# Half-size weight chunks, and a unit of its own for emptying a pair of PSUM banks

## The chip, the cores and the metric

The kernel runs on one core of a Trainium2 chip. The metric is the device time of the whole program in microseconds. TensorE is called PE here (PEld: its weight loads), VectorE DVE, ScalarE ACT, GpSimd POOL and SyncE SP, as in the profile. A granted clock of 1.00 is TensorE's upper level of 2.4 GHz, 0.50 the lower one of 1.2 GHz.

## The reference

Two transformer blocks of two layers each, on one sequence of 256 tokens by 1024 features, all in float32. The first block is a mixture of two attentions and a convolved feed-forward network (FFN); the second is an FFN, a "mix" stage and another FFN. Cut to the second block, where most of the steps below lie:

```python
for l in range(2):                                   # second_block
    x = x + 0.5 * swiglu(rms_norm(x, n1[l]), w_gate1, w_up1, w_down1)     # 1024 -> 2816 -> 1024
    proj = rms_norm(x, nm[l]) @ w_in[l] + b_in[l]
    q, k, v, f_logit, xr, gr, g_attn, g_rnn = split(proj)
    y_attn = forgetting_attention(norm(q), norm(k), v, log_sigmoid(f_logit)) @ w_o_attn[l]
    yr = rg_lru(causal_conv(xr), ...) * gelu(gr)      # sigmoid gates, then a scan over the tokens
    y_rnn = yr @ w_o_rnn[l]
    x = x + (sigmoid(g_attn) * y_attn + sigmoid(g_rnn) * y_rnn) @ w_out[l]
    x = x + 0.5 * swiglu(rms_norm(x, n2[l]), w_gate2, w_up2, w_down2)
```

## The kernel before

**Weights.** All weights, about 330 MB, are read once, in one fixed order (`stream`, built by `phase_chunks`). A chunk is 128 partitions by 2048 float32, 1 MB. `issue_dma` (L250) loads a chunk into one of NRAW = 3 raw buffers (L240) from SP's queue, in one transfer, or in two of 512 KB for the row chunks of the down projections. Each product is made out of two or three products of parts, for which every weight is split in two: ACT writes the high part `wh` (`piece_h`, L275), DVE the rest `wl` = raw - wh (`piece_l`, L289), in NP = 4 pieces of 128x512 a chunk. The parts lie in rings of RING = 3 chunks each. `h_open` (L271) lets the split run up to two chunks ahead of the chunk that was taken last (`next_chunk`, L321, sets `done`). A raw buffer is free for the next load when DVE has made the last piece of it.

**Order of work.** The program is unrolled in Python and its order on each engine is written out when it is built. The PE stream is written by straight code (`proj2`, `vpair`, `down2` and so on). Between two products `substep` calls `urgent` (at least one piece of split for the next chunk), `tick` and `fill` (more split if an estimate of the engines' times allows it). `tick` (L350) goes through `active`, a list of units: generators that issue the work of ACT, DVE and POOL on a result (attention rows, gates, emptying of PSUM). A unit is resumed when its inputs are ready by the estimate and its engine is estimated to be at most CAP = 1.4 us ahead of PE, or CAPF = 4.5 us for a unit spawned with `front=True`, which also stands first in the list. Each engine runs its stream in the order so written.

**PSUM.** There are eight banks. `proj2` (L581), a product of 256 output features by 256 tokens, takes two (`wait_for(lambda: bank_any(2))`, L586); they are given back when the unit that uses the result has issued the two additions of `add_parts` (L596) or `add_bias` (L606), which sum the two halves of each bank into SBUF (ACT copies one half, DVE adds the other). That unit stands behind the older units of the list.

**An FFN of the second block.** 22 `proj2` ("up", a chunk each) make 22 tiles of the hidden layer; `evac_swiglu` (L758) turns each into an operand `as` of the down projection. `ffn_order` (L214) puts the down products in between: groups of four hidden tiles for the first 512 output features (half 0), a group when its last tile is two steps old (`lag`, 2; 4 in the first block), and after the last "up" the rest of half 0 and then all of half 1, beginning with the short group of two tiles. In the last group of a half the products are ordered by output tile, so that `boundary` (L708) can add each to `x` and make the operands `xs` of the next stage while PE goes on.

**The mix stage of the second block** (`mix2`, L1433) follows MIX2 (L235). Its later part is: G (gates of the recurrent unit), r0 to r3 and n2, n3 (`proj2` of the same input), A0 to A3, R0 to R3, O0 to O3. r0 to r3 are emptied by four `gelu_unit` (L1393), which stand in the list behind eight gate units and four `lru_unit` (L1371), the recurrence; each then waits for the recurrence, and their products `sp` are the operands of R0 to R3.

**The start.** The first four x tiles and the first two chunks are loaded in pieces of 256 KB in turn, then constants, then chunk by chunk. The squares of x for the first norm are added up on POOL (`add_squares`, L530), and a table of attention biases (`biasT`) is built by POOL's DMAs through DRAM.

Of the kernel before, what the change touches and what calls it, by code (L numbers as in the profile page):

```python
# [25 lines left out]
NG = -(-NF // 4)  # L26
NBLK = 41
# [40 lines left out]
class Estimate:  # L68
# [9 lines left out]
    def key(self, x):  # L78

        w = self.wide.get(x.name)  # L80
        return x.name if w is None else (x.name, 4 * x.offset // w)

    def cost(self, eng, op, out, ins, kw):
# [12 lines left out]
        if eng == "pool":  # L96
            return 149.0 + 2.1 * w
# [47 lines left out]
def kernel(ctx: ExitStack, tc: tile.TileContext, t: dict):  # L145
# [34 lines left out]
    def phase_chunks():  # L180
        for l in range(L):
            wo = t["w_out"]
            at = {"dq0": 0, "dq1": 1, "mq0": 2, "mq1": 3, "dv0": 4, "mv0": 5}
            for step in MIX1.split():
                if step[1] == "o":
                    stream.append(wo[l, 2 * (step[0] == "m") + int(step[2])])
                else:
                    stream.extend(t["w_p1"][l, at[step], i] for i in range(2))
            ffn_chunks(t["w_up"], t["w_down"], l, 4)
        for l in range(L):  # L190
# [3 lines left out]
            for step in MIX2.split():  # L194
                if step == "q0":
                    stream.append(t["w_qf"][l])
                elif step == "G":
                    stream.append(t["w_g"][l])
                elif step in PAIRS:
                    stream.extend(t["w_p2"][l, PAIRS.index(step), i] for i in range(2))  # L200
                elif step[0] == "O":
                    stream.append(half_rows(t["w_out2"][l], *divmod(int(step[1]), 2)))
                elif step[0] in "AR":
                    stream.append(t[{"A": "w_oa", "R": "w_or"}[step[0]]][l, int(step[1])])
                else:
                    stream.append(wi[l, base[step[0]] + int(step[1])])
            ffn_chunks(t["w_gu2"], t["w_d2"], l, 2)

    def half_rows(w, half, g):

        v = w[2 * g:min(2 * g + 2, w.shape[0])].rearrange("c p (k m) -> p c k m", k=2)
        return v[:, :, :, half * 512:(half + 1) * 512]

    def ffn_order(lag):  # L214
# [3 lines left out]
        for j in range(NF):  # L218
            yield "up", j
            while left and 4 * left[0] + 3 + lag <= j:  # L220
                yield "dn", (0, left.pop(0))
        for g in left:
            yield "dn", (0, g)
        for g in [NG - 1, *range(NG - 1)]:
            yield "dn", (1, g)

    def ffn_chunks(u, d, l, lag):
        for what, j in ffn_order(lag):
            stream.append(u[l, j] if what == "up" else half_rows(d[l], *j))
# [10 lines left out]
    NRAW = 3  # L240
    RING = 3
    NP = 4
# [7 lines left out]
    def issue_dma(parts=1, also=None):  # L250
# [7 lines left out]
        if len(stream[c].shape) == 4:  # L258
            rv = r.rearrange("p (c k m) -> p c k m", k=2, m=512)
            for i in range(rv.shape[1]):  # L260
                nc.sync.dma_start(rv[:, i], stream[c][:, i])
# [5 lines left out]
        T["dma"] = max(T["dma"], T["dve"] if c >= NRAW else 0.0) + 2900.0  # L267
# [7 lines left out]
    def piece_h():  # L275
        c, p = divmod(st["h"], NP)
        if p == 0:
            Hs[c] = wpool.tile([P, wide(c)], F32R, tag="wh", bufs=RING, name=nm("wh"))
            Ls[c] = wpool.tile([P, wide(c)], F32R, tag="wl", bufs=RING, name=nm("wl"))
            est.wide[Hs[c].name] = est.wide[Ls[c].name] = wide(c)  # L280
# [18 lines left out]
    def fill():  # L299

        issue_dma()
        while h_open() and st["h"] - st["l"] < 2 * NP:
# [9 lines left out]
    def urgent():  # L312

        if st["l"] < min((st["use"] + 1) * NP, NCHUNK * NP):
# [88 lines left out]
    for x in X:  # L403
        est.wide[x.name] = 4 * S
# [7 lines left out]
    for c in range(2):  # L412
        issue_dma(NP, lambda i: i % 2 == 0 and nc.sync.dma_start(X[2 * c + i // 2], t["x"][2 * c + i // 2]))
    for p in range(4):
        est.R[X[p].name, 0] = est.R[X[p].name, 1] = T0 - 500.0 + 2200.0 * p
    est.R[raws[0].name], est.R[raws[1].name], T["dma"] = T0 + 200.0, T0 + 4600.0, T0 + 5500.0
    nc.sync.dma_start(cst, t["cst"])
    T["dma"] += 1400.0
    issue_dma()
# [25 lines left out]
    def mm3(out, lh, ll, rh, rl, start, stop):  # L445
        pe.matmul(out, lh, rh, start=start, stop=False, skip_group_check=True)
        pe.matmul(out, lh, rl, start=False, stop=False, skip_group_check=True)
        pe.matmul(out, ll, rh, start=False, stop=stop, skip_group_check=True)

# [108 lines left out]

    def proj(R):

        h, l_ = next_chunk(None)
        h3 = h.rearrange("p (k c) -> p k c", k=KT)
        l3 = l_.rearrange("p (k c) -> p k c", k=KT)
# [3 lines left out]
        for k in range(KT):  # L567
            for m in range(2):
                ms = slice(m * P, (m + 1) * P)
                mm3(o[:, m], h3[:, k, ms], l3[:, k, ms], R.high(k), R.low(k),  # L570
# [10 lines left out]
    def proj2(R):  # L581

        h, l_ = next_chunk(None)
        h3 = h.rearrange("p (k c) -> p k c", k=KT)
        l3 = l_.rearrange("p (k c) -> p k c", k=KT)
        wait_for(lambda: bank_any(2))  # L586
        bs = [bank("mm") for _ in range(2)]
        for k in range(KT):
            for m in range(2):
                ms = slice(m * P, (m + 1) * P)  # L590
                mm2(bs[m], h3[:, k, ms], l3[:, k, ms], R.both(k), k == 0, k == KT - 1)
# [4 lines left out]
    def add_parts(t, bs):  # L596

        yield W("act", *bs)
        for m in range(2):
            act.activation(as2(t)[:, m], lo(bs[m]), AF.Copy)  # L600
        yield W("dve", t)
        for m in range(2):
            dve.tensor_add(as2(t)[:, m], hi(bs[m]), as2(t)[:, m])
            unbank()

    def add_bias(t, bs, cols):  # L606

        yield W("act", *bs)
        for m in range(2):
            act.activation(as2(t)[:, m], hi(bs[m]), AF.Identity, bias=cols[m])  # L610
        yield W("dve", t)
        for m in range(2):
            dve.tensor_add(as2(t)[:, m], lo(bs[m]), as2(t)[:, m])
            unbank()

    def vproj(R):

        h, l_ = next_chunk(None)
        h3 = h.rearrange("p (k c) -> p k c", k=KT)
        l3 = l_.rearrange("p (k c) -> p k c", k=KT)  # L620
        w = h3.shape[2]
# [4 lines left out]
        for k in range(KT):  # L626
            for m in range(2):
                ms = slice(m * P, (m + 1) * P)
                mm3(o[m], R.high(k)[:, ms], R.low(k)[:, ms], h3[:, k], l3[:, k],
# [5 lines left out]
    def vpair(R):  # L635
# [3 lines left out]
        for half in range(2):  # L639
            h, l_ = next_chunk(None)  # L640
            h3 = h.rearrange("p (k c) -> p k c", k=KT // 2)
            l3 = l_.rearrange("p (k c) -> p k c", k=KT // 2)
            for kk in range(KT // 2):
                k = half * (KT // 2) + kk
                for tt in range(2):
                    xh, xl = R.high(k)[:, tt * P:(tt + 1) * P], R.low(k)[:, tt * P:(tt + 1) * P]
                    last = k == KT - 1
                    pe.matmul(bs[tt], xh, h3[:, kk], start=k == 0, stop=False, skip_group_check=True)
                    substep()
                    pe.matmul(bs[tt], xl, h3[:, kk], start=False, stop=False, skip_group_check=True)  # L650
                    pe.matmul(bs[tt], xh, l3[:, kk], start=False, stop=last, skip_group_check=True)
                    if not (last and tt):
                        substep()
        return bs

    def down(acc, R, first, last, after=None):

        h, l_ = next_chunk(None)
        h3 = h.rearrange("p (k c) -> p k c", k=2)
        l3 = l_.rearrange("p (k c) -> p k c", k=2)  # L660

        def one(k, m):
            ms = slice(m * P, (m + 1) * P)
            mm3(as2(acc[m // 2])[:, m % 2], h3[:, k, ms], l3[:, k, ms], R.high(k), R.low(k),
                first and k == 0 and m % 2 == 0, last and k == 1 and m % 2 == 1)

        if not last:
            for k in range(2):
                for mh in range(2):
                    for m in range(4 * mh, 4 * mh + 4):  # L670
                        one(k, m)
                        substep()
        else:
            for p in range(4):
                for k in range(2):
                    for m in (2 * p, 2 * p + 1):
                        one(k, m)
# [6 lines left out]
    def down2(acc, R, ks, half_, first, last, after):  # L684

        h, l_ = next_chunk(None)
# [1004 lines left out]
```

## Time and profile before

| | us |
|---|---|
| median of 3 runs | 1897.28 |
| lowest and highest | 1894.22, 1897.31 |
| the profiled execution, its own time | 1893.61 |
| span in its profile | 1891.8 |
| PE busy | 1857.2 |
| ACT busy | 1258.8 |
| DVE busy | 1523.7 |

The span runs from the first to the last instruction; 1.8 us lie around it. PE's busy time is 98% of the span. Matmuls overlap, so one that takes 395 ns by itself costs less in a row of them, and the time of a stage is best read from the chain of work that ended last, where the pieces add up. A profile line names its instruction by its tiles: `mm` and `acc` are PSUM banks, `wh` and `wl` the parts of the weights, `ge` the emptied banks of r0 to r3.

### The profile page before, as it was taken

To read this page: it belongs to the slowest core of one execution; us is meant where nothing else is said; L and a number is where in the kernel's file an instruction comes from. 1 tells how busy PE (TensorE), PEld (TensorE's weight loads), DVE (VectorE), ACT (ScalarE), POOL (GpSimd) and SP (SyncE) were. 2 spreads that over 40 slices of the span, in tenths; PEclk is the share of its full clock that TensorE was granted. 3 is DMA by queue.
4 is the path that set the end of the run, shared out by engine and by line. 5 is a ranking of instruction groups with operands and counts; after the bars stand their busy time and mean duration, and the time that the engine had idled before them with its cause. 6 is when DMAs were issued, how large, how long until landed. Compare 5 with 4: busy or idle time off the path is not lost.

```text
span 1891.8 us, 31179 instructions
## 1 busy us (share of the span) xinstructions
PE 1857.2 (98%) x11446; PEld 1652.2 (87%) x11446; DVE 1523.7 (81%) x3301; ACT 1258.8 (67%) x3123; POOL 69.0 (4%) x98
## 2 busy tenths in 40 slices
PE   8999999999999999999989999999999999899999
PEld 6799998889999888888878888888888888788888
DVE  6889887888988777779977987787777897888775
ACT  6777565877656656567786665566556678866653
POOL 3010001001000000010000100010000000000000
PEclk9999999999999999999998999999999999899999
DMA  9435555443554655464454555555546445455543
GB/s 268 153 113 182 198 168 204 142 157 134 201 179 152 227 195 184 167 227 164 169 179 163 182 189 199 167 201 192 198 156 247 167 156 179 170 184 191 191 157 133
DMA packets 79161, 339.68 MB, mean 180 GB/s; under 512 B 7020, under 2 KB 8084, under 8 KB 48288
## 3 DMA queue, kind: packets, MB, share of 16 engines
q1 hardware_dynamic: 77408, 330.20, 51.1%
q0 software_dynamic: 1456, 7.47, 1.3%
q8 instruction: 90, 1.47, 0.3%
q14 instruction: 63, 0.52, 0.1%
q10 hardware_dynamic: 144, 0.02, 0.0%
HBM read 336.30 MB, written 1.36 MB: 178 GB/s over the span
## 4 chain that ended last, share of the span: by engine, by line
PE 92%; ACT 3%; DVE 3%; DMA 2%; issue 0%; SPq 0%; ACTq 0%
PE mm L112 51%; PE acc L112 23%; PE mv L112 13%; DMA raw<-in_w_p 2%; PE av L112 1%; DVE wl L112 1%; PE s L112 1%; ACT wh L112 1%; PE qt L112 1%; PE pt L112 1%; ACT r L112 1%; ACT th L112 1%; DVE xs L112 0%; DVE z L112 0%; DVE yc L112 0%
## 5 line engine op out<-in xcount | busy, mean ns | idle before, releaser
L112 DVE TENSOR_TENSOR wl<-raw,wh 128x512 fp32r<-128x512 f32 x1272 | 816.2, 678 | 142.0 <-ACT wh L112 132.6
L112 ACT ACTIVATE wh<-raw 128x512 fp32r<-128x512 f32 x1272 | 702.2, 617 | 201.5 <-PE acc L112 85.7
L112 PE MATMUL mm<-xs,wh 128*128 128x256 f32 (+1 forms) x2816 | 745.5, 339 | 2.8 <-DVE xs L112 2.8
L112 PE MATMUL mm<-xs,wl 128*128 128x256 f32 x2112 | 591.4, 280 | 0.0
L112 PEld LDWEIGHTS mm<-xs,wh 128*128 128x128 f32 x2816 | 483.6, 189 | 64.4 <-DVE xs L112 3.6
L112 PEld LDWEIGHTS mm<-xs,wl 128*128 128x128 f32 x2112 | 399.7, 189 | 0.1
L112 PE MATMUL acc<-as,wh 128*128 128x512 f32 x1056 | 369.8, 395 | 0.0
L112 PE MATMUL acc<-as,wl 128*128 128x256 f32 x1056 | 294.9, 279 | 0.0
L112 PE MATMUL mv<-wh,xs 128*128 128x512 f32 (+2 forms) x832 | 255.2, 384 | 0.0
L112 PEld LDWEIGHTS acc<-as,wh 128*128 128x128 f32 x1056 | 198.4, 188 | 46.1
L112 PE MATMUL mm<-hS,wh 128*128 128x512 f32 x512 | 185.8, 406 | 16.7 <-DVE ge L112 16.7
L112 PEld LDWEIGHTS acc<-as,wl 128*128 128x128 f32 x1056 | 199.3, 189 | 0.0
L112 PEld LDWEIGHTS mv<-wh,xs 128*128 128x128 f32 x832 | 149.7, 189 | 26.2 <-ACT xs L112 0.6
L112 PE MATMUL mv<-wl,xs 128*128 128x512 f32 (+2 forms) x416 | 156.1, 375 | 0.0
L112 DVE TENSOR_TENSOR u<-mm,u 128x256 f32<-128x256 f32 x176 | 67.5, 424 | 100.8 <-ACT u L112 100.8
L112 PE MATMUL mm<-hS,wl 128*128 128x256 f32 x512 | 145.1, 283 | 0.0
L112 ACT ACTIVATE u<-mm 128x256 f32<-128x256 f32 x176 | 63.7, 384 | 117.2 <-PE mm L112 116.9
L112 PEld LDWEIGHTS mm<-hS,wh 128*128 128x128 f32 x512 | 98.6, 193 | 40.0 <-issue 17.3
L112 POOL TENSOR_TENSOR sq<-sq,sq 128x256 f32<-128x256 f32 x70 | 55.7, 796 | 1578.1 <-ACT sq L112 1576.3
L112 PEld LDWEIGHTS mm<-hS,wl 128*128 128x128 f32 x512 | 99.0, 193 | 0.1
L112 ACT ACTIVATE as<-u 128x256 fp32r<-128x256 f32 x88 | 36.3, 416 | 82.3 <-DVE u L112 82.3
L112 PEld LDWEIGHTS mv<-wl,xs 128*128 128x128 f32 x416 | 78.5, 189 | 13.3 <-DVE wl L112 0.3
(209 smaller groups left out, 2279.4 us busy)
## 6 DMA issues: line engine op xcount, KB each, us to landing
raw<-in_w_gu SPq DMA_DIRECT2D x88, 1024.0 KB, 4.9
raw<-in_w_up SPq DMA_DIRECT2D x44, 1024.0 KB, 4.9
raw<-in_w_d SPq DMA_DIRECT2D x88, 512.0 KB, 4.6
raw<-in_w_p SPq DMA_DIRECT2D x42, 1024.0 KB, 5.3
raw<-in_w_in SPq DMA_DIRECT2D x34, 1024.0 KB, 4.9
raw<-in_w_down SPq DMA_DIRECT2D x44, 512.0 KB, 4.5
raw<-in_w_out SPq DMA_DIRECT2D x8, 1024.0 KB, 4.9
raw<-in_w_oa SPq DMA_DIRECT2D x8, 1024.0 KB, 4.8
```

Of the source, the lines that this page charges most:

```text
L112: f(*a, **k)
```

## The change

Chunks are halved: every chunk of the stream becomes two of 128x1024 (512 KB, one transfer each), split in NP = 2 pieces of 128x512. NRAW becomes 7 and RING 5, both in half chunks, and the limits of `fill` and `urgent` are doubled in halves, so that they are the same in pieces. Products take the halves one after the other through a generator, `k_chunks`; where the products are ordered by output tile, all halves of the group are taken at once with `list`. The groups of an FFN's down projection are of two hidden tiles instead of four (NG = 11), except the last of half 1, which has two groups at once; half 1 begins with group 0.

`add_parts` and `add_bias` go away. `summed` spawns a unit of its own, with `front=True`, that empties the two banks of a `proj2`; the unit that uses the result polls until it is there.

The squares of the first norm are added on DVE, the pool of working tiles has 43 buffers instead of 41, and the estimate's numbers for POOL and for loads are adapted.

```diff
-NG = -(-NF // 4)
-NBLK = 41
+NG = NF // 2
+NBLK = 43
+    def halves(a):
+        w = a.shape[-1] // 2
+        stream.extend(a[:, i * w:(i + 1) * w] for i in range(2))
...
     def half_rows(w, half, g):
-        v = w[2 * g:min(2 * g + 2, w.shape[0])].rearrange("c p (k m) -> p c k m", k=2)
-        return v[:, :, :, half * 512:(half + 1) * 512]
+        return w[g].rearrange("p (k m) -> p k m", k=2)[:, :, half * 512:(half + 1) * 512]
     def ffn_order(lag):
         left = list(range(NG))
         for j in range(NF):
             yield "up", j
-            while left and 4 * left[0] + 3 + lag <= j:
-                yield "dn", (0, left.pop(0))
+            while left and 2 * left[0] + 1 + lag <= j:
+                yield "dn", (0, (left.pop(0),))
         for g in left:
-            yield "dn", (0, g)
-        for g in [NG - 1, *range(NG - 1)]:
-            yield "dn", (1, g)
+            yield "dn", (0, (g,))
+        for g in range(NG - 2):
+            yield "dn", (1, (g,))
+        yield "dn", (1, (NG - 2, NG - 1))
...
-    NRAW = 3
-    RING = 3
-    NP = 4
+    NRAW = 7
+    RING = 5
+    NP = 2
...
-        while h_open() and st["h"] - st["l"] < 2 * NP:
+        while h_open() and st["h"] - st["l"] < 4 * NP:
...
-        if st["l"] < min((st["use"] + 1) * NP, NCHUNK * NP):
+        if st["l"] < min((st["use"] + 2) * NP, NCHUNK * NP):
...
-            pool.tensor_add(N.ss[0], N.ss[0], sq)
+            (dve if N is norms[0] else pool).tensor_add(N.ss[0], N.ss[0], sq)
...
+    def k_chunks(n=KT, c=2):
+        per = n // c
+        for i in range(c):
+            h, l_ = next_chunk(None)
+            h3 = h.rearrange("p (k c) -> p k c", k=per)
+            l3 = l_.rearrange("p (k c) -> p k c", k=per)
+            for j in range(per):
+                yield i * per + j, h3[:, j], l3[:, j]
...
-    def add_parts(t, bs):
...
-    def add_bias(t, bs, cols):
...
+    def summed(name, bs, cols=None):
+        x = Box()
+        x.t = blk(name)
+        def unit():
+            yield W("act", *bs)
+            for m in range(2):
+                if cols is None:
+                    act.activation(as2(x.t)[:, m], lo(bs[m]), AF.Copy)
+                else:
+                    act.activation(as2(x.t)[:, m], lo(bs[m]), AF.Identity, bias=cols[m])
+            yield W("dve", x.t)
+            for m in range(2):
+                dve.tensor_add(as2(x.t)[:, m], hi(bs[m]), as2(x.t)[:, m])
+                unbank()
+            x.ready = True
+        spawn(unit(), front=True)
+        return x
...
     def down2(...)
-            for m in range(4):
-                for i in range(len(ks)):
-                    one(i, m)
+            w = list(k_chunks(n, len(groups)))
+            for m in range(4):
+                for i, h, l_ in w:
+                    one(i, m, h, l_)
...
-    def gelu_unit(b, j, l, R):
-        ge = blk("ge")
-        yield from add_bias(ge, b, [v1(("bin", l), 32 + 2 * j + m) for m in range(2)])
-        while R.nh < 4:
+    def gelu_unit(x, j, l, R):
+        while not x.ready or R.nh < 4:
             yield POLL
+        ge = x.t
...
-                spawn(gelu_unit(proj2(H_), j, l, R))
+                spawn(gelu_unit(summed("ge", proj2(H_), bias(32 + 2 * j)), j, l, R))
```

## Rows read from the trace of the kernel before

**Rows 1.** the page's span, and its part 1: busy time, share of the span, instructions.
```profile
span 1891.8 us, 31179 instructions
...
PE 1857.2 (98%) x11446; PEld 1652.2 (87%) x11446; DVE 1523.7 (81%) x3301; ACT 1258.8 (67%) x3123; POOL 69.0 (4%) x98
```

**Rows 2.** waits of PE, whole span: what waited for what, us in total, times, longest.
```profile
PE mm L112 <- DVE ge L112: 16.7, 2, 8.4
PE qt L112 <- DVE qn L112: 7.2, 1, 7.2
```

**Rows 3.** windows of 40 us: busy time (instructions) by engine, granted clock, DMA share, GB/s.
```profile
0.00:40.00 40.00, 36.67 (x161) 29.87 (x162) 26.67 (x60) 29.56 (x111) 15.72 (x29) 1.00 0.92 271
40.00:80.00 40.00, 32.66 (x181) 26.09 (x180) 29.21 (x92) 31.80 (x140) 0.00 (x0) 0.91 0.59 169
960.00:1000.00 40.00, 31.63 (x187) 27.93 (x186) 27.76 (x52) 38.52 (x80) 0.00 (x0) 0.91 0.47 161
```

**Rows 4.** the chain of work that ended last: start us, us, what.
```profile
758.25 22.19 PE mm L112 x128
780.43 38.83 PE acc L112 x224
...
996.72 59.55 PE mm L112 x320
...
1623.40 58.63 PE mm L112 x320
```

**Rows 5.** windows of 2 us, PE alone: busy (instructions), granted clock, DMA share, GB/s.
```profile
990.00:992.00 2.00, 0.00 (x0) 1.00 0.50 209
992.00:994.00 2.00, 0.00 (x0) 0.67 0.55 102
```

**Rows 6.** timeline of ACT, 930 to 1045: start, us, instruction.
```profile
991.80 3.01 ACT L112 ACTIVATE ge<-mm,vec 128x256 f32<-128x256 f32 x8
```

**Rows 7.** timeline of DVE, the same stretch.
```profile
996.16 2.07 DVE L112 TENSOR_TENSOR ge<-mm,ge 128x256 f32<-128x256 f32 x6
...
1014.60 1.10 DVE L112 TENSOR_TENSOR sp<-ge,sp 128x256 fp32r<-128x256 f32 x3 [0.88 <-ACT sp L112]
```

**Rows 8.** windows of layer 0's mix stage: columns as in Rows 3.
```profile
960.00:988.40 28.40, 28.36 (x177) 25.11 (x175) 16.26 (x31) 27.96 (x60) 0.00 (x0) 1.00 0.47 157
988.40:996.70 8.30, 0.00 (x0) 0.01 (x1) 8.23 (x15) 7.32 (x17) 0.00 (x0) 0.76 0.64 238
996.70:1015.70 19.00, 18.98 (x91) 16.43 (x92) 14.80 (x33) 15.06 (x31) 0.00 (x0) 0.84 0.24 71
```

**Rows 9.** groups of ACT's instructions from 960 to 1015.7: count, busy, mean ns.
```profile
L112 ACT ACTIVATE wh<-raw 128x512 fp32r<-128x512 f32 x32 | 18.3, 639 | 0.0
```

**Rows 10.** timeline of ACT, then DVE, at the last hidden tile of an FFN.
```profile
780.12 0.73 ACT L112 ACTIVATE u<-mm 128x256 f32<-128x256 f32 x2 [1.63 <-PE mm L112]
...
784.07 0.42 DVE L112 TENSOR_TENSOR as<-u,as 128x256 fp32r<-128x256 f32 x1 [0.48 <-ACT as L112]
```

**Rows 11.** the page's DMA issues: count, KB each, median us to landing.
```profile
raw<-in_w_gu SPq DMA_DIRECT2D x88, 1024.0 KB, 4.9
...
raw<-in_w_d SPq DMA_DIRECT2D x88, 512.0 KB, 4.6
```

**Rows 12.** GB/s of all DMA in 40 equal slices of the first 20 us.
```profile
GB/s 0 0 0 16 116 393 357 347 373 177 275 375 346 279 298 307 320 328 324 328 377 406 414 393 422 406 451 434 475 344 475 375 377 422 482 364 475 393 426 459
```

**Rows 13.** the start: the chain's DMA piece, then POOL's additions and its DMA behind them.
```profile
31.04 15.75 DMA raw<-in_w_p
...
15.39 6.28 POOL L112 TENSOR_TENSOR sq<-sq,sq 128x256 f32<-128x256 f32 x7 [9.40 <-ACT sq L112]
...
21.63 0.64 POOL L960 DMA_DIRECT2D ext<-mk  x1
```

**Rows 14.** timeline of ACT in the last group of an FFN's half 1.
```profile
813.63 2.20 ACT L112 ACTIVATE wh<-raw 128x512 fp32r<-128x512 f32 x4 [3.30 <-PE acc L112]
816.42 0.51 ACT L112 ACTIVATE xs<-x,vec 128x256 fp32r<-128x256 f32 x1 [0.59 <-DVE x L112]
```

More of the change, by code (lines that the diff above doesn't have):

```diff
@@ L257, in issue_dma @@
         w = wide(c) // parts
[L258 to L261, printed above, removed]
+        if len(stream[c].shape) == 3:
+            nc.sync.dma_start(r.rearrange("p (k m) -> p k m", k=2), stream[c])
         else:
@@ L638, in vpair @@
         bs = [bank("mv") for _ in range(2)]
[L639 to L648, printed above, removed]
+        for k, h, l_ in k_chunks(c=4):
+            for tt in range(2):
+                xh, xl = R.high(k)[:, tt * P:(tt + 1) * P], R.low(k)[:, tt * P:(tt + 1) * P]
+                last = k == KT - 1
+                pe.matmul(bs[tt], xh, h, start=k == 0, stop=False, skip_group_check=True)
+                substep()
+                pe.matmul(bs[tt], xl, h, start=False, stop=False, skip_group_check=True)
+                pe.matmul(bs[tt], xh, l_, start=False, stop=last, skip_group_check=True)
+                if not (last and tt):
@@ L673, in down @@
         else:
+            w = list(k_chunks(2))
             for p in range(4):
-                for k in range(2):
+                for k, h, l_ in w:
                     for m in (2 * p, 2 * p + 1):
-                        one(k, m)
+                        one(k, m, h, l_)
                         if k == 0:
@@ L736, in ffn @@
             if what == "up":
-                spawn(evac(N, mul(R), j, A.tiles))
+                b = mul(R)
+                spawn(evac(N, b if mul is proj else summed("u", b), j, A.tiles))
                 substep()
             else:
-                half_, g = j
-                ks = range(4 * g, min(4 * g + 4, NF))
-                wait_for(lambda: all(A.tiles[k] is not None for k in ks))
+                half_, groups = j
+                wait_for(lambda: all(A.tiles[2 * g + i] is not None for g in groups for i in range(2)))
                 first = not acc[half_]
@@ L746, in ffn @@
                     acc[half_] = [bank("acc") for _ in range(4)]
-                down2(acc[half_], A, ks, half_, first, g == NG - 1 - half_, boundary(scale, N2))
+                down2(acc[half_], A, groups, half_, first, NG - 1 in groups, boundary(scale, N2))
     def finish_act(av, j, tiles):
@@ L756, in finish_act, with evac_swiglu @@
         tiles[j] = a
-    def evac_swiglu(N, bs, j, tiles):
-        u = blk("u")
-        yield from add_parts(u, bs)
-        while N.rstd is None:
+    def evac_swiglu(N, x, j, tiles):
+        while not (x.ready and N.rstd is not None):
             yield POLL
+        u = x.t
         yield W("dve", u, N.rstd)
@@ L1316, in forget_unit, with xr_unit @@
         yield from split_out(b, out, m)
-    def xr_unit(b, j, l, R):
-        x2 = blk("xr")
-        yield from add_bias(x2, b, [v1(("bin", l), 24 + 2 * j + m) for m in range(2)])
+    def xr_unit(x, j, l, R):
+        while not x.ready:
+            yield POLL
+        x2 = x.t
         yield W("act", x2)
@@ L1359, in gate_unit, with sig_unit @@
         R.ng += 1
-    def sig_unit(b, cols, box, ready):
-        box.s = blk("sg")
-        yield from add_bias(box.s, b, cols)
-        while not ready():
+    def sig_unit(x, box, ready):
+        while not (x.ready and ready()):
             yield POLL
+        box.s = x.t
         yield W("act", box.s)
@@ L1412, in split_pair, with ya_unit @@
             tiles[2 * j + m] = a
-    def ya_unit(b, sg, M, j):
-        u = blk("ya")
-        yield from add_parts(u, b)
-        while not sg.ready:
+    def ya_unit(x, sg, M, j):
+        while not (x.ready and sg.ready):
             yield POLL
+        u = x.t
         yield W("dve", u, sg.s)
@@ L1421, in ya_unit, with yr_unit @@
         M.t[j] = sg.s
-    def yr_unit(b, sg, M, j):
-        u = blk("yr")
-        yield from add_parts(u, b)
-        while M.t[j] is None or not sg.ready:
+    def yr_unit(x, sg, M, j):
+        while M.t[j] is None or not (x.ready and sg.ready):
             yield POLL
+        u = x.t
         yield W("dve", u, sg.s)
@@ L1527, in mix2 @@
                     acc[half_] = [bank("acc") for _ in range(4)]
[L1528 removed]
+                down2(acc[half_], Ops(M.m), (2 * g, 2 * g + 1), half_, g == 0, g == 1, boundary(1.0, N2))
             substep()
```

156 lines of the change are left out of this document (65 added, 91 removed).

## The prediction

> **What bounds the kernel now.** I read the page's busy shares first. PE is busy 1857.2 of 1891.8 us, DVE and ACT 81% and 67% [rows 1]. So PE is the bound nearly everywhere, and all that a change of order can give is PE's 34.6 us of idle time and what a lower clock costs around it. The waits of PE say where the idle time is: 16.7 us in two waits of matmuls on DVE's `ge`, and 7.2 us in one wait of a transpose on `qn` [rows 2]; the other 10.7 us are the start, the end and small waits. The windows put them in their stages: 3.3 us idle in 0 to 40, where DMA has a share of 0.92, 7.3 us in 40 to 80 and 8.4 us in 960 to 1000, the last two with a granted clock of 0.91 [rows 3]. The wait of 960 to 1000 comes again in layer 1, 627 us later: it is the second block's mix stage.
>
> There the chain runs through ACT and DVE and comes back to PE at 996.72 and 1623.40 [rows 4]. PE wants to begin n2 and has no bank: r0 to r3 hold all eight. ACT is busy 27.96 of 28.4 us before [rows 8] and empties all eight banks in one go at 991.80 [rows 6], DVE adds from 996.16 on [rows 7], though r0 had ended some 17 us before the stall (three products of 5.55 us; 22.19 us for 128 matmuls is four of 32 [rows 4]). The emptying was not slow, it stood behind the gates and the recurrence in the order written out.
>
> Then the clock: while PE stands idle it is still 1.00 from 990 to 992 and 0.67 from 992 to 994 [rows 5], so it went to its lower level in the midst of the wait, and the matmuls after it run slower. The 320 matmuls from the restart to the O products should take 320 x 22.19 / 128 = 55.48 us; they took 59.55 and 58.63 [rows 4]. So the clock costs 4.07 and 3.15 us more.
>
> **The change part by part.**
>
> *Emptying as a front unit.* In `tick` the sums of r0 now come ahead of gates and recurrence, with a limit of 4.5 us instead of 1.4. A pair costs ACT 3.01 / 4 = 0.75 us and DVE about 0.7 us (2.07 us for six additions) [rows 6, 7]; with a few us of queue r0's banks are free about 5 us after r0's end, 12 us before n2 wants them. The wait goes: 2 x 8.37 = 16.7 us, and with it the clock's 7.2 us: 23.9 us. No work is added; ACT does 3 us of it earlier and the recurrence that much later.
>
> What is late next is R0, which needs `sp`. Unstalled, PE reaches it six products after 988.4: 988.4 + 33.3 = 1021.7. `sp` was whole at 1014.60 + 1.10 = 1015.7 [rows 7]. By then ACT must also have split two more chunks, A3 and R0: 8 pieces at 18.3 / 32 = 0.57 us, 4.6 us [rows 9]. ACT was idle 55.7 - 27.96 - 7.32 - 15.06 = 5.4 us of this stretch [rows 8], much of it waiting for the late n2. So `sp` comes between 1015.7 (the idle time takes it all) and 1020.3 (none of it): 1.4 to 6 us to spare. I take no wait, and keep half of the gain lost as a rival.
>
> *Groups of two hidden tiles.* PE's products are the same in number and shape; only their order moves. In the second block (lag 2) one group of half 0 still lies between the last "up" and the group that needs its tile: before a group of four tiles, 16 pairs of matmuls, now one of two, 8 pairs, 2.77 us. The tile's chain begins at 780.12 and ends at 784.07 + 0.42 = 784.49 [rows 10], 4.06 us after PE's down products began at 780.43 [rows 4]. The second pair of the last group wants it at 2.77 + 0.35 = 3.12 us. PE waits 0.94 us, in four FFNs 3.8 us. The front unit may shorten the chain by a little and a split piece in between lengthen it: from 0 to 2.1 us each (two pieces of about 0.6 more), 0 to 8.5 us. In the first block (lag 4) two short groups lie between, as long as the one before: nothing.
>
> *Half chunks.* In pieces the look-ahead is the same (four halves ahead for two chunks); pieces fall from 1272 to 1248, since the short groups were split in 256 columns; ACT and DVE save a few us beside PE's work, nothing on the path. The loads double in number from SP, which does nothing else: nothing, as long as transfers of 512 KB keep up. They do in the down stage, which already uses them, landing in 4.6 us against 4.9 us for 1 MB [rows 11], without a wait of PE over 38.83 us [rows 4].
>
> In the last group of half 1 both halves are taken at once, so the ring opens the fifth half ahead, whose buffer is that of the first, in use to the group's end. ACT takes such pieces at once (before it waited 3.30 us for PE on one, and `xs` stands behind it [rows 14]); now it could stand there for most of the group's 5.55 us, with `xs` and `sq`, DVE's `wl` and the SP load that wants that raw buffer behind it. In the FFN ends this moves the four last `xs` by about 2.5 us (from 816.42 to some 818.9, where 15 of the group's 16 pairs are done); PE wants the first of them 2.8 us (8 pairs of 0.35) into the next stage, so most is covered. Between 0 and 3.5 us at each of nine places (five FFN ends, two mix stages, two ends of the first block's attention): 0 to 31 us. I take 2 us, because the first half's `xs` are long there and cover the start.
>
> *The start.* The chain there is a load of 15.75 us [rows 13], so DMA sets it, among POOL's table DMAs. The seven additions of squares move from POOL (6.28 us [rows 13]) to DVE (7 x 0.42 [rows 10], 2.9 us, between its splits); POOL's `ext`, queued behind them to 21.63 us, goes some 3 us earlier, and half a chunk more is on its way. DMA was busy for 0.92 of the first 40 us [rows 3], 3.2 us short of all of it, and that much at most is there to be filled. Bounds: 3 us lost (DVE's split, which now stands behind additions that wait for ACT's squares), 11 us won (the whole wait of 7.2 [rows 2] and the clock's part of the next window, 0.09 x 40 = 3.6 [rows 3]). I take 2 won.
>
> Sum from the profiled execution's 1893.6: - 23.9 + 3.8 + 2 - 2 = 1873.5. It was 3.7 below the median of 1897.3, so I forecast a median of **1877**, and 1870 to 1886 for this case alone.
>
> One rule speaks against the change: the Trainium skill, DMA: Bandwidth & Descriptors, section Bandwidth, says to batch DMAs to 1 MiB or more for three quarters of peak. By its measured rate for 1 MB a weight stage would have ample room and by half-size transfers one by one it would not. The trace disagrees for transfers in flight together: the first 20 us, with pieces of 256 KB, show up to 482 GB/s [rows 12]. By the trace the sum stays 1877; by the rule it would be the 1903 of the slow loads below.
>
> **The rivals.**
> *Half the gain is taken by ACT.* In 960 to 996.7 ACT is full [rows 8]; if R0 or a weight piece waits instead, half the idle time and half the clock's loss stay: 1877 + 12 = 1889 (1883 to 1897). For: the full engine. Against: the spare time above.
> *The start clears too.* The 11 us instead of 2: 1868.
> *The ring in pairs (slower).* ACT blocked at the ends of stages as told; at 3.5 us in all nine places 31.5 instead of 2: 1906. It decides from where a place costs (1897.3 - 1877 + 2) / 9 = 2.5 us. Against: 2.8 us of cover in block two.
> *Half-size loads are slower (slower).* Bound from rows: two transfers one after the other, 2 x 4.6 - 4.9 = 4.3 us a chunk, in the six whole chunks of the DMA-bound start 26 us: 1903. Against: [rows 12]. This is where the skill's rule above would lead.
> *It doesn't do what it says.* The sums stand in front of the list but are still issued late, since ACT is over its limit: 23.9 us stay, 1901.
>
> **How the numbers follow.** Forecast 0.64, half the gain 0.15, the start too 0.09, the ring 0.06, slow loads 0.02, no effect 0.04. 0.2% is 3.8 us, about what a measurement of this kernel can tell from no change. Faster (under 1893.5): 0.64 + 0.09 + 0.11 of the half gain = 0.84. Within: 0.04 of it, 0.02 of no effect, 0.01 of the ring, 0.07. Slower: 0.09. The range 1863 to 1893 takes in the forecast with its unknown costs, most of the cleared start and most of the half gain; the slower cases stay out.
>
> **What the profile of after would show.** No wait of `mm` on `ge`; `ge` copies of ACT in pairs, each soon after its product; a clock of 1.00 through both mix stages; the chain from n2 to the O products at 55.5 us. A wait of `acc` on `as` of about 1 us, four times, right after 22 "ups". At the ends of stages, waits of ACT's `wh` on PE of up to 5 us and, if the ring decides, waits of `mm` or `mv` on `xs`. In the start, `ext` by 19 us and a shorter wait on `qn`. I am wrong if PE waits on `sp` or on `wl` in the mix stage, or if the ends of stages show waits of PE over 2.5 us.

## The result, and the profile of the changed kernel

| | before | after |
|---|---|---|
| median, us | 1895.75 | 1906.82 |
| lowest and highest | 1894.20 to 1897.31 | 1904.00 to 1911.04 |
| the profiled execution's span | 1891.8 | 1902.2 |

The change makes the kernel slower by 0.6%: a ratio of 1.006, 95% interval 1.0038 to 1.0082. The forecast was 1877, and its range ended at 1893.

Where the time went is seen best by stage. In PE's timeline a stage begins with its first matmul behind the last `acc` of the stage before. The columns of three experiments, told below, stand beside the two kernels already: `e1` is the changed kernel with the ring counted in another way, `e2` the kernel before with the front sums alone, `e10` the best version.

| stage, us | before | after | e1 | e2 | e10 |
|---|---|---|---|---|---|
| start and first attention | 136.8 | 129.1 | 133.7 | 139.6 | 127.3 |
| first block, FFN 0 | 191.2 | 191.7 | 189.4 | 191.2 | 188.2 |
| first block, attention 1 | 116.4 | 121.5 | 116.1 | 116.3 | 116.1 |
| first block, FFN 1 | 191.2 | 191.8 | 189.4 | 191.2 | 188.3 |
| second block, layer 0, first FFN | 183.6 | 188.6 | 185.9 | 183.6 | 184.6 |
| layer 0, mix | 259.6 | 253.6 | 249.3 | 248.3 | 247.7 |
| layer 0, second FFN | 183.5 | 190.3 | 185.9 | 187.1 | 184.6 |
| layer 1, first FFN | 183.5 | 190.3 | 185.9 | 183.6 | 184.6 |
| layer 1, mix | 258.7 | 252.6 | 249.6 | 248.3 | 248.0 |
| layer 1, second FFN | 183.4 | 188.7 | 185.8 | 183.5 | 184.5 |

So the start and the two mix stages won 7.7 + 6.0 + 6.1 = 19.8 us, and nearly everything else lost: the four FFNs of the second block 5 to 7 us each, 23.8 in all, the second attention 5.1, the FFNs of the first block 0.5 each. A wait of PE in front of the first matmul of a stage is counted with the stage before it.

Where PE stood, by the waits of PE in the changed kernel (what waited for what, us in total, times, longest):

```profile
PE st L112 <- POOL sq L112: 12.8, 7, 2.4
PE acc L112 <- DVE as L112: 5.4, 6, 1.1
PE mm L112 <- DVE xs L112: 4.8, 6, 1.2
PE mm L112 <- DVE sp L112: 2.6, 2, 1.3
PE mm L112 <- ACT xs L112: 2.0, 2, 1.0
...
PE qt L112 <- DVE qn L112: 2.0, 2, 1.7
```

Against [rows 2] the wait on `ge` is gone and the one on `qn` is 2.0 instead of 7.2. In their place stands `st`, the matmul that adds up the squares for a norm. It stood 7 times for the sum of squares behind the end of a stage, where the kernel before did so once in all, for 1.3 us, in the start. Behind the two other ends, those of the first block's attentions, PE stood 1.0 and 1.2 us for `xs`. PE's busy time rose too, and busy time that grows with the same matmuls is a lower clock or a slower pace (page, part 1; [rows 1]):

```profile
PE 1865.8 (98%) x11446; PEld 1657.9 (87%) x11446; DVE 1534.8 (81%) x3284; ACT 1271.2 (67%) x3099; POOL 63.5 (3%) x91
```

**One end of a stage, closely.** The first FFN of layer 0 in the second block ends at 822.66, with the last pair of halves taken at once. First ACT's timeline there (start, us, instruction, in brackets the idle time before it and what ended it):

```profile
817.73 0.62 ACT L112 ACTIVATE wh<-raw 128x512 fp32r<-128x512 f32 x1
822.05 1.16 ACT L112 ACTIVATE wh<-raw 128x512 fp32r<-128x512 f32 x2 [3.70 <-PE acc L112]
823.11 0.49 ACT L112 ACTIVATE xs<-x,vec 128x256 fp32r<-128x256 f32 x1
...
828.10 0.40 ACT L112 ACTIVATE sq<-x 128x256 f32<-128x256 f32 x1
```

DVE's timeline, the same stretch:

```profile
822.71 0.69 DVE L112 TENSOR_TENSOR wl<-raw,wh 128x512 fp32r<-128x512 f32 x1 [2.77 <-PE acc L112]
823.32 0.88 DVE L112 SCALAR_TENSOR_TENSOR x<-acc,x 128x256 f32<-128x256 f32 x2
...
827.57 1.29 DVE L112 SCALAR_TENSOR_TENSOR xs<-x,vec,xs 128x256 fp32r<-128x256 f32 x2
```

And PE's:

```profile
829.71 0.70 PE L112 MATMUL st<-sq,cst 128*128 128x256 f32 x2 [2.04 <-POOL sq L112]
```

ACT began a piece of the fifth half ahead, whose buffer the running group was still reading, and stood 3.70 us; DVE did the same with its part, 2.77 us. Six of the eight additions to `x`, all four `xs` and their squares stood in line behind these pieces. The last `xs` was done at 827.57 + 1.29 = 828.86, 6.2 us into the new stage, and POOL's last sum of squares at 829.66; `st` stood in PE's order from 827.67 on. In the kernel before the same `xs` were done 3.1 us into the stage (820.90 + 1.31 against 819.10):

```profile
820.90 1.31 DVE L112 SCALAR_TENSOR_TENSOR xs<-x,vec,xs 128x256 fp32r<-128x256 f32 x2
```

and POOL's last sum of squares at 822.24 + 0.75 = 822.99:

```profile
822.24 0.75 POOL L112 TENSOR_TENSOR sq<-sq,sq 128x256 f32<-128x256 f32 x1
```

PE's `st` started at 823.10, without a wait:

```profile
823.10 0.64 PE L112 MATMUL st<-sq,cst 128*128 128x256 f32 x2
```

The margin there was 0.1 us, so a delay of about 3 us had nowhere to go. (PE came to `st` 1.0 us later in the changed kernel, after three more matmuls and a wait of 0.19 us for an `xs`; the other 2.0 us it stood.) The clock follows, in windows of the changed kernel, all engines (busy us of PE, PEld, DVE, ACT, POOL, the granted clock, DMA share, GB/s):

```profile
822.00:834.00 12.00, 9.77 (x63) 9.21 (x62) 9.41 (x17) 9.63 (x20) 3.86 (x5) 0.86 0.52 175
828.00:830.00 2.00, 0.29 (x1) 0.30 (x2) 1.81 (x3) 2.00 (x6) 1.51 (x3) 1.00 0.48 185
830.00:832.00 2.00, 2.00 (x11) 1.95 (x11) 2.00 (x4) 1.97 (x4) 0.00 (x0) 0.61 0.99 320
832.00:834.00 2.00, 2.00 (x12) 2.00 (x11) 0.41 (x2) 1.84 (x5) 0.00 (x0) 0.53 0.96 349
834.00:836.00 2.00, 2.00 (x19) 2.00 (x19) 1.93 (x5) 0.40 (x2) 0.00 (x0) 1.00 0.93 287
```

The clock falls here after the idle time, not in it: 1.00 while PE stands, then 0.61 and 0.53, near the lower level, while it works again. 11 and 12 matmuls in 2 us instead of 19: the 15 that are missing are 1.6 us more, on top of the 2.0 us of waiting.

In this execution the clock fell at six of the nine ends of stages and stayed at 1.00 at three, though PE waits 2.0 to 2.4 us in all at each. Two waits of `st` of 1.62 us, up to 640.87 and up to 1083.12, show both cases in the windows behind them:

```profile
641.00:645.00 4.00, 4.00 (x23) 3.51 (x24) 2.93 (x6) 3.97 (x9) 0.00 (x0) 1.00 0.46 142
1083.00:1087.00 4.00, 3.88 (x13) 3.29 (x14) 2.70 (x5) 3.55 (x7) 0.07 (x1) 0.57 0.40 121
```

The mix stage did what was forecast. ACT empties r0 to r3 at 980.64, 986.70, 992.42 and 996.69, each pair for itself, instead of all eight banks at once [rows 6]:

```profile
980.64 0.92 ACT L112 ACTIVATE ge<-mm,vec 128x256 f32<-128x256 f32 x2
```

PE is busy through the windows where it stood before, with a clock of 1.00 [rows 3]:

```profile
40.00:80.00 40.00, 37.93 (x236) 29.54 (x235) 35.48 (x114) 35.10 (x150) 0.00 (x0) 1.00 0.60 181
960.00:1000.00 40.00, 40.00 (x246) 35.81 (x245) 25.60 (x51) 36.53 (x79) 0.00 (x0) 1.00 0.53 176
```

### The profile page after: what moved, and what is told of

Read it like the earlier page. It is cut to its first block, busy times and chain, and to the rows that moved or that the text cites. A ratio compares the mean times of both kernels' runs of the same rounds, so it can differ in the third digit from the quotient of the medians.

```text
span 1902.2 us, 32094 instructions
## 1 busy us (share of the span) xinstructions
PE 1865.8 (98%) x11446; PEld 1657.9 (87%) x11446; DVE 1534.8 (81%) x3284; ACT 1271.2 (67%) x3099; POOL 63.5 (3%) x91
## 4 chain that ended last, share of the span: by engine, by line
PE 89%; DVE 7%; ACT 2%; DMA 1%; issue 1%; POOL 0%; POOLq 0%; SPq 0%; ACTq 0%
PE mm L112 49%; PE acc L112 22%; PE mv L112 12%; DVE wl L112 2%; PE av L112 2%; PE s L112 1%; DMA raw<-in_w_p 1%; ACT wh L112 1%; DVE x L112 1%; PE qt L112 1%; PE pt L112 1%; PE g L112 1%; DVE xs L112 1%; DVE z L112 0%; PE st L112 0%
## 5 line engine op out<-in xcount | busy, mean ns | idle before, releaser
L112 ACT ACTIVATE wh<-raw 128x512 fp32r<-128x512 f32 x1248 | 718.3, 628 | 317.0 <-PE mm L112 101.7
L112 PE MATMUL mm<-xs,wh 128*128 128x256 f32 (+1 forms) x2816 | 753.4, 340 | 6.8 <-DVE xs L112 4.8
L112 PE MATMUL mm<-hS,wh 128*128 128x512 f32 x512 | 180.9, 395 | 0.0
L112 POOL TENSOR_TENSOR sq<-sq,sq 128x256 f32<-128x256 f32 x63 | 50.2, 797 | 1578.4 <-ACT sq L112 1577.1
L112 DVE SCALAR_TENSOR_TENSOR y<-u,vec,y 128x255 f32<-128x255 f32 (+1 forms) x176 | 80.8, 481 | 3.1
```

Of the source, the lines that this page charges most:

```text
L112: f(*a, **k)
```

## The experiments

Theory 1: the clash of the ring at the ends of stages costs about 27 us. Theory 2: the halves and the short groups themselves do. The ratio given with each kernel is to runs of the kernel before on the same chip, 95% interval in brackets.

**The ring counted from the first half of a running group.**

```diff
             w = list(k_chunks(n, len(groups)))
+            st["done"] = st["use"] - len(groups)
...
             w = list(k_chunks(2))
+            st["done"] = st["use"] - 2
```

> The changed kernel, but while a group that takes all its halves at once is running, the ring counts from the first of them, so the split opens one half less ahead and never a buffer that the running group still reads. Theory 1 (the ring in pairs): in the changed kernel PE waits 12.8 us on POOL's sq for the matmul st and 6.8 us on xs, of which the kernel before had 1.3 and 2.8, and at each of some seven stage ends the lower clock costs about 1.7 us more. All of it goes: 15.5 + 12 = 27 us, a time of 1880 (1873 to 1888), no wait of ACT's wh on PE's acc over 1 us at a stage end, st's waits under 3 us in all. Theory 2 (it is the halves and the short groups themselves: more transfers, more starts of chunks, a shorter cover for the last hidden tile): stage ends stay as they are, 1900 to 1908.

Measured: 1876.05 us, a ratio of 0.990 [0.989, 0.992], where the changed kernel had 1.006. Theory 1. All three waits of the ends of stages are gone; what is left of PE's waits:

```profile
PE acc L112 <- DVE as L112: 5.4, 6, 1.1
PE qt L112 <- DVE qn L112: 4.0, 1, 4.0
PE mm L112 <- DVE sp L112: 2.6, 2, 1.3
...
PE st L112 <- DVE sq L112: 1.2, 1, 1.2
PE mm L112 <- DVE xs L112: 0.2, 1, 0.2
```

The `st` that is left is the start's. In the 12 us around the same end of a stage PE issued 99 matmuls instead of 63, at a clock of 1.00 (windows of this kernel, columns as above):

```profile
814.00:826.00 12.00, 12.00 (x99) 11.81 (x98) 10.27 (x21) 9.32 (x18) 2.80 (x4) 1.00 0.72 274
```

At this pace 36 matmuls are 4.4 us. 12 - 9.77 = 2.2 of them are idle time; the rest is the lower clock and what it costs to start again. By the table of stages the nine stages behind the start are shorter than in the changed kernel by 2.3, 5.3, 2.4, 2.7, 4.3, 4.3, 4.4, 3.0 and 2.9, 31.5 us in sum, 3.5 us for each of the nine places. By places, with the wait of 1.0 us in front of each FFN of the first block moved to where it belongs, the first three are 3.3, 4.3 and 3.4. The three places where the clock stayed at 1.00 are the cheapest, 2.7, 3.0 and 2.9; with a lower clock a place costs 3.3 to 4.4. Of the whole, some 32 us by places, 20 are waits (12.8 on `sq`, 4.8 + 2.0 + 0.4 on `xs`).

**The front sums alone,** in the kernel before: `add_parts` and `add_bias` replaced by `summed` and the users as in the change, nothing else.

> The kernel before with one part of the change alone: the two banks of a pair are emptied by a unit of its own, ahead of the other background work. Theory A (what the prediction said of the mix stage): the two waits on ge (16.7 us) and the clock behind them (7.2 us) go, and R0 then waits about 1.3 us twice, as in the changed kernel: 1896.5 - 23.9 + 2.6 = 1875 (1869 to 1882), the FFNs as before. Theory B (the smaller pieces of the halves were needed for it, or the front units delay the split in the FFNs): 1886 or more, with a wait on ge of over 2 us left or new waits of mm on wl.

Measured: 1877.42 us, 0.991 [0.990, 0.993]. Theory A. The mix stages are shorter by 11.4 and 10.4 us, and the waits of PE have no `ge` and no `sp`:

```profile
PE qt L112 <- DVE qn L112: 9.3, 1, 9.3
PE mm L112 <- DVE xs L112: 2.7, 4, 0.9
...
PE st L112 <- POOL sq L112: 1.3, 1, 1.3
```

R0 waits for `sp` only where the chunks are halved as well. The halves were not needed for this gain. Without halves the start's wait stays.

**The sums behind the other work,** in the changed kernel:

```diff
-        spawn(unit(), front=True)
+        spawn(unit())
         return x
```

> The changed kernel, but the unit that empties a pair of banks stands at the end of the list, with the limit of 1.4 us, as the sums stood in the kernel before. Theory A: the waits on ge come back, two of about 8 us with their clock, and the small waits on sp go: 1907 + 21 = 1928 (1922 to 1934). Theory B (the front sums cost in the FFNs about what they give in the mix stage): 1900 to 1912, with shorter waits of acc on as (5.4 us in all) and of st on sq (12.8 us).

Measured: 1914.26 us, 1.010 [1.009, 1.012], 7 to 8 us above the changed kernel in spans, ratios and medians (4.0 by the stages behind the start, which took 3.6 us more in this profile), where theory A expected 15 to 27 and theory B next to nothing: neither. The waits on `ge` came back, but shorter:

```profile
PE mm L112 <- DVE ge L112: 8.5, 6, 2.8
```

ACT emptied r0 at 1001.17, between pieces of split, and r1 and r2 at 1002.92, not all eight banks together (its timeline):

```profile
1001.17 0.82 ACT L112 ACTIVATE ge<-mm,vec 128x256 f32<-128x256 f32 x2
...
1002.92 1.56 ACT L112 ACTIVATE ge<-mm,vec 128x256 f32<-128x256 f32 x4
```

So the halves take away half of the stall without the front unit. That they do it by breaking up the order of ACT's work is how this timeline reads; which of their parts does so was not tried.

**The same, with the ring mended** (both edits above).

> The kernel e1_ring_held with the unit that empties a pair of banks at the end of the list, as in e3_sums_behind: the halves alone, without the clash of the ring. If the two parts add up: e1_ring_held plus the 10 us that e3_sums_behind stood above the changed kernel, 0.9955 of the kernel before, some 1884 to 1889, with waits of mm on ge of about 8.5 us in all instead of the 16.7 before. Rival (the stall of the mix stage was short in e3_sums_behind only since the stage before ended late): the 16.7 us come back, 1898 or more.

Measured: 1883.43 us, 0.994 [0.993, 0.996], with 6.7 us of waits on `ge`. Taking the front unit away costs 8 us here and 4 to 8 with the clash, so the clash changes little of what it is worth. The halves and the front sums overlap: the halves with the ring mended are worth some 11 us, the front sums by themselves some 17, both together 18.6, since the halves take away part of the same stall.

**The squares of the first norm on POOL again,** in the changed kernel:

```diff
-            (dve if N is norms[0] else pool).tensor_add(N.ss[0], N.ss[0], sq)
+            pool.tensor_add(N.ss[0], N.ss[0], sq)
```

> The changed kernel, but the seven additions of squares of the first norm are on POOL again. The changed kernel is 8 to 10 us ahead of the one before when the first FFN begins. Theory S (POOL's queue sets the start: additions, then ext and the table that the first attention waits for): the wait of qt on qn is 6 us or more again, and the time 1907 + 8 = 1915 (1911 to 1918). Theory L (it is the loads: halves issued in another order, one more on its way): the start stays, 1905 to 1909.

Measured: 1904.08 us, 1.006 [1.004, 1.008], the time of the changed kernel. Theory S fails: the gain of the start does not hang on the squares. That it is the loads', as theory L says, is left over by this run and not shown by it. POOL's `ext` is issued at 21.67, as late as before [rows 13], and yet `qt` hardly waits:

```profile
PE qt L112 <- DVE qn L112: 0.3, 1, 0.3
```

**One more buffer in the ring:** NRAW = 5 and RING = 6 in the changed kernel.

> The changed kernel with six buffers of each part instead of five and five raw buffers instead of seven; the ring is counted as in the changed kernel. Theory 1 (it is the counting: the split opens as far ahead as there are buffers, so the last one opened is always that of the running group's first half): the clash stays, only one half later, and what stands behind it a little less: waits of st on sq of 5 to 13 us in all, 1890 to 1906. Theory 2 (five buffers were simply too few): the clash goes, st's waits under 2 us, 1876 to 1882. Theory 3 (raw buffers are what is short): worse than the changed kernel, waits on wl appear, over 1912.

Measured: 1911.63 us, 1.010 [1.008, 1.012], above theory 1's range; but by what it has on the clash theory 1 holds. ACT stands as long as before (its timeline at the same end of a stage):

```profile
835.11 1.15 ACT L112 ACTIVATE wh<-raw 128x512 fp32r<-128x512 f32 x2 [3.74 <-PE acc L112]
```

and PE's waits on the sum of squares and on `qn`:

```profile
PE st L112 <- POOL sq L112: 9.6, 5, 2.4
PE qt L112 <- DVE qn L112: 6.7, 1, 6.7
```

A sixth buffer does not remove the clash, since the split opens as far ahead as there are buffers: of the nine places seven keep it, and only behind the two mix stages is no wait of `st` or `xs` left. Behind the start the kernel takes as long as the changed one (1768.5 us from the first matmul of the first FFN to the last `acc`, against 1769.2). The whole loss is in the start, 138.2 us to the first FFN instead of 129.1; two fewer raw buffers are the likely reason, but this run changes two numbers at once.

**`st` later.** In the changed kernel, 4 us later in PE's order by the estimate:

```diff
         yield W("pe", ssum)
+        t0 = T["pe"]
+        while N is not norms[0] and T["pe"] < t0 + 4000.0:
+            yield POLL
```

> The changed kernel, ring as it is, but PE's matmul st, which takes the sum of the squares of the norm, is written about 4 us later into PE's order for all norms but the first. What failed in the prediction by theory 1: it counted the cover for the first xs of the next stage, and not st, which stands fixed in PE's order a few us into the stage and needs all eight squares. Then the 12.8 us of st's waits go and most of the lower clock behind them (some 1.7 us at seven places), while waits on xs stay at 5 to 8 us: 12 to 24 us less than the changed kernel, 0.994 to 1.000 of the kernel before. Rival (PE would wait in any case, since what it needs next, xs, the split pieces or the banks that wait for rstd, is as late): the waits move to xs, wl or u, and the time is within 6 us of the changed kernel, 1.003 to 1.008.

Measured: 1893.80 us, 0.9986 [0.9977, 0.9995]: 13 us less than the changed kernel, at the lower end of what theory 1 expected. The waits of `st` at the ends of stages are gone, and matmuls on `xs` wait more often, 1.2 us at the longest:

```profile
PE mm L112 <- DVE xs L112: 8.8, 14, 1.2
...
PE mm L112 <- ACT xs L112: 2.0, 2, 1.0
...
PE mv L112 <- DVE xs L112: 1.6, 4, 0.6
```

So somewhat under half of the clash's price (13 of 31 us) hung on the place of one matmul; with `st` out of the way PE meets the late `xs` themselves, one by one. The granted clock is 1.00 from 100 us to 1880, so the clock's part of the price is gone with the longer waits.

**One more group behind the last up,** on `e1_ring_held`: `lag` 6 for 4 in the first block, 4 for 2 in the second.

> The kernel e1_ring_held (ring counted from the first half of a running group), and in each FFN one more group of two hidden tiles lies between the last up and the group that needs its tile (lag 6 instead of 4 in the first block, 4 instead of 2 in the second). Theory 1 (cover: the last tile's chain takes 6 to 7 us and the groups of two leave 2.8 us less in the second block): the six waits of acc on as, 5.4 us in all, go; e1_ring_held stood at 0.990 of the kernel before, this one is 5 us less, 0.9875, some 1869 to 1873 us. Theory 2 (the chain itself grows with what is put between, split pieces first): part of the wait stays, 2 us or more, and the time is that of e1_ring_held, within 2 us.

Measured: 1866.13 us, 0.985 [0.983, 0.988]. Theory 1: no wait of `acc` on `as` is left, and each FFN is shorter by 1.2 to 1.4 us. What the wait was, in the chain of `e1_ring_held` behind the last up (start us, us, what):

```profile
776.86 0.37 ACT u L112
...
777.48 0.63 ACT wh L112
...
778.14 0.69 DVE wl L112
778.83 0.60 DVE u L112
779.43 0.60 DVE wl L112
...
780.85 0.44 DVE as L112
...
781.33 33.43 PE acc L112 x190
```

Two pieces of DVE's split, 0.69 and 0.60 us, stand inside the tile's chain.

**The gates one product earlier,** on `e5_ring_lag`: "a3 n0 G n1 r0" in MIX2.

> The kernel e5_ring_lag, and in the second block's mix stage the gates G come one product earlier, ahead of n1 instead of behind it, so that the recurrence can start 5.5 us earlier. Theory A (R0's wait of 1.3 us on sp, twice, is the end of the recurrence's chain): the wait goes, 2 to 3 us less than e5_ring_lag. Theory B (ACT's whole load sets the time of sp, not when the gates come): the same time as e5_ring_lag within 1.5 us, the waits on sp stay. Theory C (G now waits for the convolution's yL): PE waits on yL, slower by some us.

Measured: 1864.94 us, 0.985 [0.983, 0.987], the time of `e5_ring_lag`. In its own stage theory A holds: no wait on `sp`, and the mix stages are 1.6 and 1.5 us shorter. The start, the same in both kernels, took 133.9 instead of 130.2 us in this profile, so the profiles can't show the gain of 3 us in the whole, and the medians don't either.

**All of it, with the squares on POOL.**

> The kernel e8_gates_early with the seven additions of squares of the first norm on POOL again: ring counted from the first half of a running group, one more group behind the last up, gates one product earlier. If the start's wait of qt on qn (4.4 us in e8_gates_early, 1.8 in e5_ring_lag, whose start is the same; 0.3 in e4_start_pool) follows the squares, it falls under 1 us and the time to 0.982 of the kernel before; if it is only the loads' luck of one execution, the time is that of e8_gates_early, 0.985, and below both kernels in any case.

Measured: 1860.61 us, 0.982 [0.981, 0.984]: 1.8% faster than the kernel before, 2.4% than the changed one. The start's wait on `qn` is 0.3, and PE is busy in 76.4 of the first 80 us, against 69.3 [rows 3]. Seven profiles with the squares on DVE and seven raw buffers took 129.1 to 133.9 us to the first FFN, the two with them on POOL 127.3 both times. Two pairs of kernels differ in nothing else. The changed kernel and `e4_start_pool` show no difference (1.006 both); `e8_gates_early` and `e10_best` are 0.985 and 0.982 of the kernel before, with intervals that touch. So adding the squares on DVE gained nothing; whether it costs 0 or 5 us is open.

## Why the prediction was wrong

**What bounds, and the mix stage: right.** The 23.9 us were read from idle time and clock, and the front sums alone gave 21.8 (11.4 + 10.4). The sign that was asked for is there: `ge` in pairs and a clock of 1.00. "I take no wait" of R0 was right for the sums alone and 1.3 us too low twice where the halves are in as well. Together with the halves the mix stages won 10.3 and 9.1 us once the ring is mended.

**The ring: the step that failed.** The prediction saw the mechanism: the fifth half opened into the first half's buffer, ACT and DVE standing in it, `xs` behind them, at nine places. It bounded a place at 0 to 3.5 us, and put the sum of the bad case at 31.5; measured are 31.5. That the sums agree is luck: the bound held no clock, and four of the places cost 4.3 or 4.4. What it took was 2, because "PE wants the first of them 2.8 us into the next stage, so most is covered". Three things are wrong in that sentence. It looked at the first `xs` only; PE also needs all eight squares, for `st`, whose place in PE's stream was written out before. The margin behind it could be read in the trace of before, though no view of waits shows it: the last sum of squares ended at 822.99, `st` began at 823.10, 0.1 us. The delay of the last `xs` was put at 2.5 us and was 3.1 (from 3.1 to 6.2 us into the stage). And no clock was counted, though [rows 5] had shown what a long wait does: of 4.4 us at the place told above about half is not idle time. The sign of being wrong, waits over 2.5 us at the ends of stages, left the clock out too, and the longest wait there was 2.4. The rival, "the ring in pairs", had 1906 and a chance of 0.06. The point from which it decides, 2.5 us for each place, was passed at all nine. That it met the time so closely is in part chance: the start came out 5.7 and the rest of the first block 3.8 us better than forecast, the mix stages 4.5 and the FFNs of the second block, without the ring, 5.8 worse.

The Trainium skill, PSUM — Partial Sum Buffer, section Engine vs sequencer instructions, says that matmuls start and complete in program order. The trace agrees: PE stood 2.04 us in front of `st`, though the last `xs` was done 0.85 us before it, and `e9_st_later`, with `st` written later, won 13 us.

**The groups of two: mechanism right, size low.** 0.94 us each in the four FFNs of the second block was forecast, 1.0 to 1.1 came. "In the first block nothing" was wrong: 0.7 each. Four pieces of 128x512 (1.28 and 1.29 us on DVE for two) stand in the chain of the last tile there, where the kernel before had four of 128x256 in its short group (1.09 for three, 0.42 for one), and from `u` to `as` the chain takes 6.5 us instead of 5.4. The bound for pieces in between was given for the second block alone.

A term was missing: PE's pace in the second block. Chain of the changed kernel:

```profile
743.42 2.81 PE acc L112 x16
746.23 11.14 PE mm L112 x64
```

Before, 64 matmuls took 22.19 / 2 = 11.10 and 16 took 38.83 / 224 x 16 = 2.77 [rows 4]. An FFN has 11 of the one and 22 of the other: 11 x 0.04 + 22 x 0.04 = 1.3 us, 5 in the four FFNs. It stays in `e5_ring_lag` and `e10_best`, at 1.0 to 1.1 by their stages. That PE pays it when it starts on another chunk is a guess that no run here tested.

**The start: sign right, size low, one of two reasons wrong.** 2 us were taken out of bounds of -3 to 11; 7.7 came in this execution, and 2.9 to 7.7 in the seven profiles with the squares on DVE and seven raw buffers, so part of the 7.7 is luck. `ext` went early as told (19.1 instead of 21.6) and this was worth nothing: the gain is there with the squares on POOL too. The front sums alone did not bring it (139.6 in `e2_sums_only`). Halves in five raw buffers did not either (138.2 in `e7_ring6`, which changes the ring too), so the other reason, that more is on its way, fits; no run changes the number of raw buffers alone.

**Half-size loads: right.** A load of 512 KB lands in 3.7 to 4.6 us by the page, and in `e1_ring_held` the waits of PE show none for a split piece, where a late load would come out. The rule of the Trainium skill that the prediction named (DMA: Bandwidth & Descriptors, section Bandwidth: batches of 1 MiB or more) does not decide here: the kernel with halves, short groups and the mended ring, without the front unit, is 0.994 of the one with whole chunks, and 1.8% are won with halves in. That halves one by one would be too slow is an estimate from [rows 11], 512 KB in 4.6 us or 114 GB/s, against the 178 GB/s that the kernel before reads over its span; the loads did not run one by one, since 596 of them at 3.7 to 4.6 us by the page are more than the span.

**The sum, put right:** 1891.8 of span - 7.7 (start) - 19.4 (mix) - 3.8 (the other three stages of the first block, by `e1`) + 9.6 (second block's FFNs: tail and pace) + 31.5 (ring) = 1902.0, against a span of 1902.2. The sum closes because the ring's term is the changed kernel less `e1`; that the terms are what they are called rests on the runs above, except for the start, whose size changes from profile to profile, and the 3.8 of the first block.

## What to carry to other kernels

When buffers get smaller and more, look for every place that holds several of them at once: a ring counted from the newest one taken opens buffers that are still being read, and one buffer more left the clash at seven of nine places. An engine that runs ahead into such a buffer blocks all that stands behind it, so ask what PE needs last from that queue, not first, and read its margin from the trace (the end of the producer against the start of the consumer, even where no wait is shown). A bound of 0 to 31 us is a reason to look at one of the places closely before choosing an end.

## What the hardware showed

One execution of the sums alone ran a whole FFN 2% slower at a granted clock of 1.00, with no wait: 187.1 instead of 183.5 us. Its chain, against 22.19 in [rows 4] for the same work:

```profile
1110.38 22.62 PE mm L112 x128
```

Its twin in layer 1 took 183.5. The granted clock does not show this, and a stage of one profile is not exact to better than that.

In the first block the halves go the other way: the two FFNs are shorter by 1.8 us each in `e1_ring_held` than before, in spite of the tail's wait of 0.7, with the same matmuls. A part of it is idle time. The kernel before waits for `xs` near the start of these FFNs, 0.5 and 0.9 us in each, `e1_ring_held` only 0.2 once. What makes up the rest, some 1.2 us in each, is open.
